# Retention branch product as seven block products per head, with tokens on partitions and the heads' sum kept on chip

## The chip, the cores and the metric

The kernel runs on one core of a Trainium2 chip. The metric is the device time of one execution in microseconds; the median of three executions before the change is 1123.46 us (1120.56 to 1124.0). A core has a matrix engine (TensorE, PE in the profile), three engines for elementwise work (VectorE or DVE, ScalarE or ACT, GpSimdE or POOL), a queue engine (SyncE, SP), and DMA engines that move data between the chip's memory and the on-chip buffers (SBUF for operands, PSUM for matmul results). Every engine works through its own instructions in the order in which they stand in its queue. In this kernel SP and POOL issue the DMAs.

## The reference

One layer of a decoder: 512 tokens, model width 1024, all fp32. A retention branch with four heads and an attention branch read the same normalised input. Cut to what the change touches:

```python
proj = h @ w_in                                  # rq, rk, rv, rg, ..., gr, gm
ro = retention(rope(rq), rope(rk) * 256**-0.5, rv)   # 4 heads, values 512 wide
ro = rms_norm(ro, ret_norm)                      # over the 512 of a head
a_ret = (ro * silu(rg)) @ w_br                   # (512 x 2048) @ (2048 x 1024)
...
mixed = sigmoid(gr) * a_ret + sigmoid(gm) * a_mla
x = x + mixed @ w_o
x = x + square(relu(rms_norm(x) @ w_up)) @ w_down
```

For one head, the branch product is a 512x512 block of `ro * silu(rg)` (tokens by values) times a 512x1024 block of `w_br`, and the four heads' products are summed.

## The kernel before

**Tiles.** Activations lie with features on the partitions and the 512 tokens along the free axis: a tile is 128x512. An fp32 product is made of three fp32r matmuls (`mm3`: high part times high part and the two mixed terms). So every operand is split into a high and a low part: ACT makes the high part by a copy (line 306 for activations, 261 for weights), DVE subtracts it for the low part (line 307 for activations, 265 or 267 for weights).

**Weights.** They come in 512 KB chunks of 128x1024. `prepare` issues a chunk's DMA on SP into one of six raw buffers (`wr_...`, line 233 or 243), `load_chunk` splits it into `wh_...` and `wl_...` (three buffers each). The list of steps in the kernel's main function sets the order of the matmuls; `run_steps` calls `load_chunk` one step ahead of use and `prepare` three further steps ahead. PE executes in the order of the list. Where the instructions of ACT, DVE, SP and POOL stand relative to one another is decided when the program is built, by a scheduler.

**Seven products.** The values (`ret_v`, tiles rv), the gates (`ret_gate`, tiles rg) and the MLP's second product cut both operands in 2x2 blocks and make the result from seven block products instead of eight, numbered 1, 7, 2, 6, 5, 4, 3 in order of use. The weights' block sums are made by DMA: the first block is loaded into a raw buffer by SP, and POOL issues a DMA that adds another block to it in place (line 223). Products 7, 6 and 4 use one raw buffer: product 6's weights are product 7's plus one more block, product 4's are product 6's plus one more. So the addition for product 6 can be issued when product 7's weights have been split, and the addition for product 4 when product 6's have. Products 1, 6, 5, 3 are accumulated in one PSUM area (chain a: the result is read out after each of them), 7 and 4 in a second one, 2 in a third one (`CHAIN`). `seven_out` reads them out: ACT copies after products 1, 7 and 6 (tiles z.._11, z.._22, z.._21 for the gates), DVE adds after 2, 5 and 4.

**Order of one head.** rq and rk (two chunks each), for even heads rv (14 chunks, values of two heads), the branch product of the previous head, gates 1 and 7, scores (`ret_scores`, tiles rs and s), gates 2 and 6, `ret_attend` (tiles ath and atl are the split scores, ro the result, og its scaled copy), gates 5, 4 and 3. During heads 0 and 2 the gate's products stand between rv or the branch product and the next head's rq.

**Branch product before.** `ret_factor` broadcasts the norm's factor of each token over the partitions with four small transposes (tile pbo), multiplies and splits the gated result into `rog`. `branch_r` makes eight output tiles of 128 features by 512 tokens, in four chunks of `w_br`, each tile of 4 x 3 matmuls of 128x512. For heads 0 to 2, ACT copies each tile (line 861) and a DMA on POOL writes it to (head 0) or adds it into (heads 1, 2) a buffer in the chip's memory, `ret{n}d`. `reload` brings the sums back as `re`, with the attention's part `ze` and the gate inputs `ge`; for head 3 DVE adds the product to `re` (line 867).

**End of the mixer.** `mix` multiplies by the gate, adds the attention's part and splits the sum into `mix{n}` (three DVE operations, lines 897, 898 and 307); `out_part` makes the first halves of two output tiles wo0 and wo1, `out_proj` the rest.

## Time and profile before

| what | value |
|---|---|
| median of three executions | 1123.46 us |
| the profiled execution | 1125.78 us |
| its span, first to last instruction | 1124.0 us |
| PE busy | 1107.5 us, 99% |
| DVE busy | 734.9 us, 65% |
| ACT busy | 536.7 us, 48% |
| weights and other reads | 156.92 MB, written 15.99 MB |

The profile gives the busy time of each engine, the chain of work that ended last (followed backwards from the last instruction), groups of equal instructions, and DMA issues with the time from issue to landing. The trace behind it gives, for each engine, a timeline: start in us, duration in us, engine, line, operation, result and operands, how often it repeats, and in brackets the idle time before it and what ended that. The line number of nearly all matmuls is that of one helper (168), so they are told apart by the tile that they write. Durations of matmuls overlap: one starts before the one ahead has ended, so the distance from start to start is what a matmul costs.

### The profile page before, as it was taken

The numbers are of one execution on the slowest core, as the hardware profiler recorded it, in microseconds if no ns is written. First come the engines' busy times: TensorE is split into PE (matmuls) and PEld (weight loads), VectorE is DVE, ScalarE is ACT, GpSimd is POOL, SyncE is SP. The second block draws the span as 40 slices with busy tenths as digits, with TensorE's granted clock in tenths as the row PEclk, the third lists the DMA queues.
The fourth block names the chain that finished last, engine by engine and source line by source line (L and its number), as shares of the span: only waits on it lengthen the run. The fifth ranks groups of instructions, "written<-read, shape, count | busy, mean of one in ns | idle before, by whom it ended". The sixth has DMA issues, their size and how long they took to land.

```text
span 1124.0 us, 14722 instructions
## 1 busy us (share of the span) xinstructions
PE 1107.5 (99%) x5549; PEld 939.0 (84%) x5549; DVE 734.9 (65%) x1206; ACT 536.7 (48%) x762; POOL 85.4 (8%) x113
## 2 busy tenths in 40 slices
PE   9999999999999999999999999999999999999998
PEld 7878878888888889888888987888888888888877
DVE  7777677556785836845483678555466666668675
ACT  7457556444465435445443644434443443445542
POOL 0000000001110020031003000010100100101000
PEclk9999999999999999999999999999999999999999
DMA  8133231356786274599529754693855755738501
GB/s 264 59 98 106 67 99 57 128 210 211 190 225 173 87 212 121 135 202 253 137 92 220 223 172 154 196 274 117 171 165 168 176 166 155 186 123 219 146 29 75
DMA packets 59223, 175.97 MB, mean 157 GB/s; under 512 B 7248, under 2 KB 8656, under 8 KB 58896
## 3 DMA queue, kind: packets, MB, share of 16 engines
q1 hardware_dynamic: 45168, 129.66, 33.8%
q0 software_dynamic: 13840, 45.36, 20.9%
q8 instruction: 43, 0.70, 0.2%
q14 instruction: 28, 0.23, 0.1%
q10 hardware_dynamic: 144, 0.03, 0.0%
HBM read 156.92 MB, written 15.99 MB: 154 GB/s over the span
## 4 chain that ended last, share of the span: by engine, by line
PE 87%; DVE 4%; DMA 4%; ACT 2%; issue 2%; SPq 0%; ACTq 0%; DVEq 0%; POOLq 0%
PE up L168 16%; PE dn L168 14%; PE br L168 6%; PE rg L168 5%; PE rv L168 5%; PE pg L168 4%; PE gr L168 4%; PE rq L168 4%; PE rk L168 4%; PE bm L168 4%; PE wo L168 4%; DMA wr_rg<-wstream 4%; PE gm L168 3%; PE ro L168 3%; PE sc L168 2%
## 5 line engine op out<-in xcount | busy, mean ns | idle before, releaser
L168 PE MATMUL dn<-wh_dn,cl 128*128 128x512 f32 x224 | 87.2, 389 | 0.0
L168 PE MATMUL dn<-wh_dn,ch 128*128 128x512 f32 x224 | 87.2, 389 | 0.0
L168 PE MATMUL dn<-wl_dn,ch 128*128 128x512 f32 x224 | 87.1, 389 | 0.0
L261 ACT ACTIVATE wh_dn<-wr_dn 128x1024 fp32r<-128x1024 f32 x32 | 34.0, 1062 | 75.5 <-PE up L168 54.3
L261 ACT ACTIVATE wh_up<-wr_up 128x1024 fp32r<-128x1024 f32 x32 | 33.9, 1061 | 57.4 <-PE up L168 29.3
L265 DVE TENSOR_TENSOR wl_dn<-wr_dn,wh_dn 128x1024 fp32r<-128x1024 f32 x32 | 39.0, 1220 | 27.5 <-ACT wh_dn L261 27.5
L265 DVE TENSOR_TENSOR wl_rg<-wr_rg,wh_rg 128x1024 fp32r<-128x1024 f32 x20 | 24.3, 1223 | 40.7 <-ACT wh_rg L261 40.4
L265 DVE TENSOR_TENSOR wl_up<-wr_up,wh_up 128x1024 fp32r<-128x1024 f32 x32 | 39.1, 1222 | 17.4 <-ACT wh_up L261 17.4
L970 DVE SCALAR_TENSOR_TENSOR f<-up,bcx 128x512 f32<-128x512 f32 x32 | 20.6, 685 | 44.1 <-PE up L168 44.1
L168 PEld LDWEIGHTS dn<-wl_dn,ch 128*128 128x128 f32 x224 | 42.0, 188 | 8.8
L168 PEld LDWEIGHTS dn<-wh_dn,cl 128*128 128x128 f32 x224 | 42.0, 188 | 8.7
L168 PEld LDWEIGHTS dn<-wh_dn,ch 128*128 128x128 f32 x224 | 42.0, 188 | 8.6
L261 ACT ACTIVATE wh_dn<-dr_dn 128x1024 fp32r<-128x1024 f32 x24 | 25.5, 1060 | 42.2 <-PE up L168 29.1
L223 POOL DMA_DIRECT2D dr_dn<-wstream x24 | 21.4, 892 | 306.3 <-DMA dr_dn<-wstream 182.0
L265 DVE TENSOR_TENSOR wl_dn<-dr_dn,wh_dn 128x1024 fp32r<-128x1024 f32 x24 | 29.3, 1222 | 22.4 <-ACT wh_dn L261 22.4
L261 ACT ACTIVATE wh_rv<-wr_rv 128x1024 fp32r<-128x1024 f32 x28 | 29.6, 1058 | 28.7 <-PE rv L168 11.8
L261 ACT ACTIVATE wh_rg<-wr_rg 128x1024 fp32r<-128x1024 f32 x28 | 29.3, 1054 | 28.9 <-DMA wr_rg<-wstream 23.6
L265 DVE TENSOR_TENSOR wl_br<-wr_br,wh_br 128x1024 fp32r<-128x1024 f32 x16 | 19.5, 1219 | 21.6 <-ACT wh_br L261 21.6
L1028 DVE TENSOR_TENSOR d<-d,dn 128x1024 f32<-128x1024 f32 x24 | 29.2, 1219 | 6.5 <-PE dn L168 6.5
L265 DVE TENSOR_TENSOR wl_rv<-wr_rv,wh_rv 128x1024 fp32r<-128x1024 f32 x20 | 24.4, 1223 | 13.6 <-ACT wh_rv L261 13.6
L861 ACT ACTIVATE rt<-br 128x512 f32<-128x512 f32 x24 | 14.3, 596 | 36.1 <-PE br L168 30.9
L644 ACT ACTIVATE p<-p,ng,hr 128x128 f32<-128x128 f32 (+3 forms) x32 | 20.6, 646 | 15.6 <-DVE ng L642 15.5
(1820 smaller groups left out, 3618.9 us busy)
## 6 DMA issues: line engine op xcount, KB each, us to landing
wr_up<-wstream SPq DMA_DIRECT2D x32, 512.0 KB, 4.4
wr_dn<-wstream SPq DMA_DIRECT2D x32, 512.0 KB, 3.4
dr_dn<-wstream POOLq DMA_DIRECT2D x24, 512.0 KB, 7.6
wr_rv<-wstream SPq DMA_DIRECT2D x20, 512.0 KB, 4.1
wr_rg<-wstream SPq DMA_DIRECT2D x20, 512.0 KB, 4.6
wr_rv<-wstream POOLq DMA_DIRECT2D x16, 512.0 KB, 6.1
wr_rg<-wstream POOLq DMA_DIRECT2D x16, 512.0 KB, 7.7
wr_br<-wstream SPq DMA_DIRECT2D x16, 512.0 KB, 3.5
```

What stands on the lines that cost most here:

```text
L168: return tc.keep_in_program_order(nc.tensor.matmul(*a, **k))
L223: nc.gpsimd.dma_start(raw, chunk(("w", blk, kb, fb, c)), accum_op=ALU.add)
L261: i = ACT(hi, raw, AF.Copy, scale=sign)
L265: TT(lo, raw, hi.bitcast(F32), op=ALU.subtract)
L644: ACT(cols[b], cols[b], AF.Exp, bias=ng[:, b:b + 1], scale=d["rq"][:, b], accum_out=sums[:, b:b + 1])
L861: ACT(t, ps, AF.Copy)
L970: STT(u[:, i], ps[:, i], 0.0, V["bcx2"], op0=ALU.max, op1=ALU.mult)
L1028: TT(to, to, dps[p], op=ALU.add if sign > 0 else ALU.subtract)
```

## The change

The operands change places: the gated retention output, tokens on the partitions of the result, becomes the stationary operand, and the weights the moving one. Each head's branch product becomes seven block products of 2 x 2 x 3 = 12 matmuls of 128x512. DVE makes the operands' block sums and splits them (`branch_operand`, two products ahead of use), and reads the result out of PSUM with one operation that multiplies by the token's factor (now a value per partition) and adds into one of eight SBUF tiles `ret[b, n]` (for head 0's first contributions ACT writes them). The weights of `w_br` come as chunks of the seven-product kind: per head five loads by SP and four adding DMAs by POOL instead of four loads. The sums stay on chip until the end, where 32 transposes on PE (`ret_turn`, tiles tr) turn them back for `mix`. To make room, the values of the odd heads are written to the chip's memory (`aside`, on POOL) and loaded again (`odd_v`, on SP, tiles cv) ahead of their use. The steps of a head's branch product are interleaved with the next head's rq and rk; head 2's rv, which had the branch product of head 1 between its chunks, now stands by itself.

```diff
-NDYN, NKEEP, NW, NRAW, NDRAW, AHEAD, PREP, EARLY, PAD = 45, 16, 3, 6, 4, 1, 3, 5, 104
+NDYN, NKEEP, NW, NRAW, NDRAW, AHEAD, PREP, EARLY, PAD = 47, 16, 3, 6, 4, 1, 3, 5, 72
...
-        for k in range(4):
-            add(("br", h, k), "w_br", _rng(h * RV, RV), _rng(2 * k * P, 2 * P))
...
+                add(("w", ("br", h), kb, fb, 0), "w_br", _rng(h * RV + kb * 256, 256), _rng(fb * S, S))
...
+                    if blk % 10 == 1:
+                        v[j] = split(t, f"rv{q}{blk}{i}")
+                        continue
+                    if blk == 12:
+                        t = T(f"cv{q}{i}_12")
+                        ACT(t, rvps[ch][i], AF.Copy)
+                    v[j] = aside(f"v{q}{j}", t)
+
+    def odd_v(h):
+        for j in range(4):
+            t = T(f"cv{h}{j}")
+            nc.sync.dma_start(t, R[h]["v"][j])
+            R[h]["v"][j] = split(t, f"rv{h}{j}")
...
+        R[h]["nr"] = sm(f"nro{h}", keep=True)
+        TS(R[h]["nr"], R[h]["r"], -1.0, None, op0=ALU.mult)
...
-    def ret_factor(h):
-        d, r = R[h], R[h]["r"]
-        bc = bcast(B(f"pbo{h}"), lambda b: r[:, b:b + 1])
-        for m in range(4):
-            TT(d["og"][m], d["og"][m], bc, op=ALU.mult)
-            new = K if m < 2 and h < RH - 1 else T
-            d["rog"][m] = split(d["og"][m], None, hi=new(f"rog{h}{m}h", F32R), lo=new(f"rog{h}{m}l", F32R))
-
-    def branch_r(w, h, half):
+    def branch_operand(h, p):
+
+        (a, b), lo_, hi_ = R[h]["o"], slice(0, 256), slice(256, 512)
+        if p == 7:
+            R[h]["s"] = T(f"bs{h}")
+        sv = two(R[h]["s"]) if "s" in R[h] else None
+        if p in (1, 2, 4):
+            src = (a if p == 1 else b)[:, :, hi_ if p == 4 else lo_]
+        elif p == 5:
+            src = two(T(f"bt{h}"))
+            TT(src, a[:, :, hi_], b[:, :, hi_], op=ALU.subtract)
+        else:
+            src = sv
+            if p == 7:
+                TT(sv, a[:, :, hi_], a[:, :, lo_], op=ALU.subtract)
+            else:
+                TT(sv, b[:, :, hi_ if p == 6 else lo_], sv, op=ALU.subtract)
+        hi, lo = two(T(f"bx{h}{p}h", F32R)), two(T(f"bx{h}{p}l", F32R))
+        split(src, None, hi=hi, lo=lo)
+        R[h]["x", p] = [(hi[:, k], lo[:, k]) for k in range(2)]
...
+    def branch_r(w, h, p):
+
+        ch, d = CHAIN[p], R[h]
+        if p in (1, 7, 2):
+            brps[ch] = [B(f"br{h}{p}{i}") for i in range(2)]
+        for k in range(2):
+            for i in range(2):
+                mm3(brps[ch][i], cut(d["x", p][k], i * P), cut(w, k * S, S), p in (1, 7, 2) and k == 0, k == 1,
+                    skip_group_check=True)
...
         for i in range(2):
-            n = 2 * half + i
-            ps = proj(B(f"br{h}{n}"), R[h]["rog"], w, i * P, 2 * P)
-            if h < RH - 1:
-                t = T(f"rt{h}{n}")
-                ACT(t, ps, AF.Copy)
-                if h == 0:
-                    ret[n] = aside(f"ret{n}", t)
-                else:
-                    nc.gpsimd.dma_start(ret[n], t, accum_op=ALU.add)
+            b, n = 2 * (to // 10 - 1) + i, to % 10 - 1
+            r, ps = d[f][:, b:b + 1], brps[ch][i]
+            if h == 0 and p in (1, 7, 6, 3):
+                ret[b, n] = T(f"ret{b}{n}")
+                ACT(ret[b, n], ps, AF.Copy, scale=r)
             else:
-                TT(ret[n], ret[n], ps, op=ALU.add)
+                STT(ret[b, n], ps, r, ret[b, n], op0=ALU.mult, op1=ALU.add)
+
+    def ret_turn(n):
+
+        trp[n] = B(f"tr{n}")
+        for b in range(4):
+            MM(trp[n][:, b * P:b * P + P], ret[b, n // 4][:, n % 4 * P:n % 4 * P + P], ident, is_transpose=True,
+               start=b == 0, stop=b == 3, skip_group_check=True)
...
-        TT(ret[n], ret[n], sgr[n], op=ALU.mult)
-        TT(ret[n], ret[n], zm[n], op=ALU.add)
-        mixed[n] = split(ret[n], f"mix{n}")
+        TT(sgr[n], trp[n], sgr[n], op=ALU.mult)
+        TT(sgr[n], sgr[n], zm[n], op=ALU.add)
+        mixed[n] = split(sgr[n], f"mix{n}")
...
+    def branch_steps(h, seq):
+
+        order = [p for p in seq if not callable(p)]
+        for p in seq:
+            if callable(p):
+                p()
+                continue
+            step(("sw", ("br", h), p, 0), branch_r, h, p)
+
+            for p2 in order[order.index(p) + 2:order.index(p) + 3]:
+                step(None, branch_operand, h, p2)
+
     for h in range(RH):
...
+        if h:
+            branch_steps(h - 1, [1, qk("rq", 1), 7, 2, qk("rk", 0), 6, 5, qk("rk", 1), 3, 4])
...
+        if h % 2:
+            step(None, odd_v, h)
...
         step(None, ret_gated, h)
+        for p in (1, 7):
+            step(None, branch_operand, h, p)
     for n in range(8):
         step(None, reload, n)
-    for n in range(EARLY, 8):
-        step(("gr", n), gate_r, n)
-        if n == EARLY:
-            step(None, ret_factor, RH - 1)
-    for k in range(4):
-        step(("br", RH - 1, k), branch_r, RH - 1, k)
-        step(None, mix, 2 * k)
-        step(None, mix, 2 * k + 1)
+    step(("gr", 5), gate_r, 5)
+    branch_steps(RH - 1, [1, 7, lambda: step(("gr", 6), gate_r, 6), 2, 6, 5, 4, 3])
+    for n in range(4):
+        step(None, ret_turn, n)
+        step(None, mix, n)
+    step(("gr", 7), gate_r, 7)
+    for n in range(4, 8):
+        step(None, ret_turn, n)
+        step(None, mix, n)
     for n in range(2):
         step(("o", n), out_part, n, 0)
```

Three places show what this does to the engines' queues. In them a name ends in the number of its buffer, and a name of the gates carries the head and the product: `wh_rg160` is the high part of head 1's weights for product 6.

The first is ACT's queue in head 1, from gate product 2's weights to the scores' splits. Before:

```order
L261 ACTIVATE wh_rg120_4257<-wr_rg120_4189 128x1024
L742 ACTIVATE z1_11_4255<-rg11_4230 128x512
L261 ACTIVATE wh_rg160_4337<-wr_rg170_4148 128x1024
L742 ACTIVATE z1_22_4289<-rg17_4264 128x512
L261 ACTIVATE wh_rg150_4371<-wr_rg150_4261 128x1024
L306 ACTIVATE ath_85<-s10_4300 128x512
L306 ACTIVATE ath_85<-s11_4311 128x384
L306 ACTIVATE ath_85<-s12_4322 128x256
L306 ACTIVATE ath_85<-s13_4333 128x256
L261 ACTIVATE wh_rg140_4474<-wr_rg170_4148 128x1024
```

The same place now, where `rv10h` to `rv13h` are the high parts of the values that were loaded again:

```order
L305 ACTIVATE rv10h_4222<-cv10_4220 128x512
L260 ACTIVATE wh_rg160_4356<-wr_rg170_4181 128x1024
L260 ACTIVATE wh_rg150_4390<-wr_rg150_4280 128x1024
L305 ACTIVATE rv11h_4228<-cv11_4226 128x512
L305 ACTIVATE rv12h_4234<-cv12_4232 128x512
L260 ACTIVATE wh_rg140_4491<-wr_rg170_4181 128x1024
L305 ACTIVATE rv13h_4240<-cv13_4238 128x512
L741 ACTIVATE z1_11_4274<-rg11_4249 128x512
L741 ACTIVATE z1_22_4308<-rg17_4283 128x512
L305 ACTIVATE ath_85<-s10_4319 128x512
```

The copy of gate product 1 (`z1_11`) stood ahead of the weights of product 6; now it, and all splits of the scores behind it, stand behind the weights of product 4 (`wh_rg140`), which are in the raw buffer only after both adding DMAs. Head 3's queue reads the same, with `z3_11` directly behind `wh_rg340`.

The four `cv` loads stand on SP among the weight loads, each behind one that waits for a raw buffer.

The second is ACT's queue in head 0, around the splits of its scores. Before:

```order
L306 ACTIVATE ath_85<-s00_3575 128x512
L306 ACTIVATE ath_85<-s01_3586 128x384
L306 ACTIVATE ath_85<-s02_3597 128x256
L261 ACTIVATE wh_rg040_3749<-wr_rg070_3459 128x1024
L306 ACTIVATE ath_85<-s03_3608 128x256
```

Now:

```order
L305 ACTIVATE ath_85<-s00_3571 128x512
L305 ACTIVATE ath_85<-s01_3582 128x384
L305 ACTIVATE ath_85<-s02_3593 128x256
L305 ACTIVATE ath_85<-s03_3604 128x256
L260 ACTIVATE wh_rg040_3743<-wr_rg070_3455 128x1024
```

The fourth split no longer stands behind product 4's weights. In head 2 it did before and still does.

The third is DVE's queue at the start of the output product, where `wl_o_1` is the low part of the second chunk of `w_o`. Before:

```order
L898 TENSOR_TENSOR re6_6376<-re6_6376,ze6_6378 128x512
L897 TENSOR_TENSOR re7_6380<-re7_6380,gr7_6506 128x512
L265 TENSOR_TENSOR wl_o_1_6700<-wr_o_1_6697,wh_o_1_6699 128x1024
L307 TENSOR_TENSOR mix6l_6688<-re6_6376,mix6h_6687 128x512
L898 TENSOR_TENSOR re7_6380<-re7_6380,ze7_6382 128x512
```

Now:

```order
L943 TENSOR_TENSOR ge4_6408<-tr4_6728,ge4_6408 128x512
L943 TENSOR_TENSOR gr5_6445<-tr5_6740,gr5_6445 128x512
L306 TENSOR_TENSOR mix3l_6692<-ge3_6404,mix3h_6691 128x512
L944 TENSOR_TENSOR ge4_6408<-ge4_6408,ze4_6406 128x512
L944 TENSOR_TENSOR gr5_6445<-gr5_6445,ze5_6410 128x512
L943 TENSOR_TENSOR gr6_6533<-tr6_6751,gr6_6533 128x512
L306 TENSOR_TENSOR mix4l_6737<-ge4_6408,mix4h_6736 128x512
L944 TENSOR_TENSOR gr6_6533<-gr6_6533,ze6_6412 128x512
L306 TENSOR_TENSOR mix5l_6748<-gr5_6445,mix5h_6747 128x512
L943 TENSOR_TENSOR gr7_6726<-tr7_6762,gr7_6726 128x512
L306 TENSOR_TENSOR mix6l_6759<-gr6_6533,mix6h_6758 128x512
L944 TENSOR_TENSOR gr7_6726<-gr7_6726,ze7_6414 128x512
L264 TENSOR_TENSOR wl_o_1_6776<-wr_o_1_6773,wh_o_1_6775 128x1024
```

Twelve operations of 512 columns, of which the first reads the transposes tr4 behind gate product 7, now stand ahead of `wl_o_1`, whose use on PE comes 12 matmuls after the last transpose (tr7).

More of the change, by code (lines that the diff above doesn't have):

```diff
@@ L566, in rotary_out @@
         for i in range(4):
[L567 removed]
+            t = dyn.tile([P, S], F32R, tag="t", name=f"qp{gq}{i}")
             for j, srct in enumerate((h1, h2, l1, l2)):
@@ L691, in branch_m @@
         zm[n] = aside(f"am{n}", t)
-    ret, sgr, mixed = [None] * 8, [None] * 8, [None] * 8
-    R = [dict(rog=[None] * 4, og=[]) for _ in range(RH)]
+    ret, sgr, mixed = {}, [None] * 8, [None] * 8
+    R = [dict() for _ in range(RH)]
     xr, xn, XS = [], [], {}
@@ L799, in ret_attend @@
         d = R[h]
+        d["o"] = [dyn.tile([P, 2, S], F32, tag="o2", name=f"og{h}{k}", bufs=2) for k in range(2)]
         for m in range(4):
@@ L869, in reload @@
+    trp = {}
+    def ret_turn(n):
[3 more added lines that the diff above has]
+               start=b == 0, stop=b == 3, skip_group_check=True)
     def reload(n):
-        for l, nm in ((ret, "re"), (zm, "ze"), (sgr, "ge")):
+        for l, nm, new in ((zm, "ze", K), (sgr, "ge", T)):
             if l is sgr and n >= EARLY:
                 continue
-            t = K(f"{nm}{n}")
+            t = new(f"{nm}{n}")
```

34 lines of the change are left out of this document (16 added, 18 removed).

## The prediction

> **What bounds the kernel now.** I read the page first, then the waits of PE, then PE's timeline in the stage that the change touches.
>
> ```profile
> span 1124.0 us, 14722 instructions
> PE 1107.5 (99%) x5549; PEld 939.0 (84%) x5549; DVE 734.9 (65%) x1206; ACT 536.7 (48%) x762; POOL 85.4 (8%) x113
> PE 87%; DVE 4%; DMA 4%; ACT 2%; issue 2%; SPq 0%; ACTq 0%; DVEq 0%; POOLq 0%
> PE ro L168 <- ACT ath L306: 2.3, 2, 1.7
> PE ro L168 <- DVE atl L307: 1.8, 2, 0.9
> PE wo L168 <- DVE wl_o L265: 0.5, 1, 0.5
> ```
>
> PE is busy 99% of the span and is 87% of the chain. So time is won by taking matmuls away, and lost wherever PE, which now waits for almost nothing, begins to wait. The waits (total, times, longest) list no wait for the branch product; in the mixer they are the two for `ro` and one for `wo`. The profiled execution took 1125.78 us, 1.78 more than its span and 2.32 more than the median of 1123.46; I sum against the first and carry the difference over to the second.
>
> **Work that PE loses and gains.**
>
> ```profile
> 396.97 21.76 PE br L168 x96
> 652.66 0.60 PE L168 MATMUL pbo<-cst,ro 128*128 128x128 f32 x4
> 653.02 0.48 PE L168 MATMUL gr<-xn0h,wl_gr 128*128 128x512 f32 x1
> 1060.83 1.75 PE tr L168 x16
> ```
>
> One head's branch product is 96 matmuls in 21.76 us, 0.227 us each (chain of waits). It becomes 7 x 12 = 84; the moving operand stays 512 wide. Four heads lose 48 matmuls: 48 x 0.227 = **-10.9 us**. The transposes of `ret_factor` go: from 652.66 to 653.02 is 0.36 us a head, **-1.4**. The 32 transposes of `ret_turn` are like the tail's `tr`, 16 in 1.75 us: **+3.5**. Work on PE: **-8.8 us**.
>
> **Head 0: a wait that goes.** The listed waits for `ro` are in heads 0 and 2, where the fourth score split stands on ACT behind product 4's weights, which wait for an adding DMA.
>
> ```profile
> 356.19 1.06 ACT L261 ACTIVATE wh_rg<-wr_rg 128x1024 fp32r<-128x1024 f32 x1 [2.19 <-DMA wr_rg<-wstream]
> 357.15 0.40 ACT L306 ACTIVATE ath<-s 128x256 fp32r<-128x256 f32 x1
> 357.60 0.38 PE L168 MATMUL ro<-ath,rv0211l 128*128 128x256 f32 x1 [0.70 <-ACT ath L306]
> 358.89 0.38 PE L168 MATMUL ro<-atl,rv0211h 128*128 128x256 f32 x1 [0.91 <-DVE atl L307]
> 434.13 7.71 PE ro L168 x48
> ```
>
> Head 1's `ro` without a wait takes 7.71 us. In head 0, from 356.63 to 357.60 and from there to 358.89 two matmuls of 0.12 take 2.26, so 2.0 to 2.1 us are lost. The queue now has all four splits ahead of those weights: **-2.1 us**. Head 2 keeps its place in the queue: **0**.
>
> **Head 1: a wait that comes.** In the order now, ACT has the copy `z1_11` behind `wh_rg140`. PE cannot begin gate product 6 before that copy, since both use one PSUM area (chain a).
>
> ```profile
> 421.69 0.60 ACT L742 ACTIVATE z<-rg 128x512 f32<-128x512 f32 x1 [1.33 <-issue]
> 431.33 1.06 ACT L261 ACTIVATE wh_rg<-wr_rg 128x1024 fp32r<-128x1024 f32 x1 [1.36 <-PE rg L168]
> 418.57 0.28 PE L168 MATMUL rg<-xn0h,wl_rg 128*128 128x256 f32 x1
> 431.08 0.28 PE L168 MATMUL rg<-s60h,wl_rg 128*128 128x256 f32 x1
> ```
>
> Before, the copy ran at 421.69, right after product 1, and the weights of product 4 were split at 431.33, released by PE: with three `wh` buffers they wait for the end of product 2. Product 6 began 431.08 - 418.57 = 12.5 us after product 1, straight after product 2. Now even with no delay by DMA, ACT after that end has `wh_rg140` (1.0), `rv13h` (0.6) and `z1_11` (0.6) to do: a **floor of 2.2 us** in which PE stands. The DMAs can add to it. Product 6's addition waits until product 7's weights are split; counting DVE's queue from rk's last matmul, that is at 0.1 us after product 1's start. Then come its landing L1, the two halves of the split (1.06 and 1.22, here 2.2), product 4's addition and its landing L2. So `wh_rg140` can start at 0.1 + L1 + 2.2 + L2, and waits beyond the floor if L1 + L2 is over 10.2.
>
> ```profile
> wr_rg<-wstream POOLq DMA_DIRECT2D x1, 512.0 KB, 6.8
> wr_rg<-wstream POOLq DMA_DIRECT2D x1, 512.0 KB, 5.5
> ...
> wr_rg<-wstream POOLq DMA_DIRECT2D x1, 512.0 KB, 5.2
> wr_rg<-wstream POOLq DMA_DIRECT2D x1, 512.0 KB, 5.3
> ...
> wr_rg<-wstream POOLq DMA_DIRECT2D x1, 512.0 KB, 8.6
> wr_rg<-wstream POOLq DMA_DIRECT2D x1, 512.0 KB, 5.8
> ...
> wr_rg<-wstream POOLq DMA_DIRECT2D x1, 512.0 KB, 8.1
> wr_rg<-wstream POOLq DMA_DIRECT2D x1, 512.0 KB, 5.5
> ```
>
> These are the pairs (product 6, product 4) of heads 0 to 3, issue to landing. Their sums are 12.3, 10.5, 14.4 and 13.6, mean 12.7. By the mean the stall is 2.2 + 2.5 = 4.7; ends 2.2 and 6.4. I take the mean, not head 1's own 10.5, because four reloads of 256 KB now share this stage: **+4.7 us**. The reloaded values `rv12`, `rv13` stand in the same queue, each behind a weight load on SP; by the sum they land about when L2 ends, and are no term of their own.
>
> **Head 3** has `z3_11` directly behind `wh_rg340`: floor 1.6, and by the same mean about **+4.7 us**. Before, heads 1 and 3 lost nothing there.
>
> **The output product: a wait that grows.** `wl_o_1` now stands behind twelve operations of `mix`, the first of which needs the transposes tr4 that follow the last gate product.
>
> ```profile
> 675.78 0.68 DVE L898 TENSOR_TENSOR re<-re,ze 128x512 f32<-128x512 f32 x1
> 676.39 0.68 DVE L897 TENSOR_TENSOR re<-re,ge 128x512 f32<-128x512 f32 x1
> 676.99 1.22 DVE L265 TENSOR_TENSOR wl_o<-wr_o,wh_o 128x1024 fp32r<-128x1024 f32 x1
> 678.12 0.68 DVE L307 TENSOR_TENSOR mix2l<-re,mix2h 128x512 fp32r<-128x512 f32 x1
> ```
>
> One such operation costs 0.60 from start to start, a weight's low part 1.13. After the gate product's end, tr4 takes 0.44 (a quarter of 1.75), the twelve 7.2, `wl_o_1` 1.2: 8.8 us. PE has tr4 to tr7 (1.75) and 12 matmuls of `wo0` (2.72): 4.5 us. Stall 4.4; before, PE lost 0.5 to 0.8 there: **+3.7 us** (ends 3 and 5).
>
> **VectorE in the branch product.** Per head DVE gets seven weight splits instead of four, seven operand splits, four subtractions and fourteen read-outs, and loses eight operations of `ret_factor`.
>
> ```profile
> 374.00:451.00 77.00, 77.00 (x449) 68.63 (x449) 46.76 (x80) 35.02 (x50) 7.91 (x12) 1.00 0.50 148
> ```
>
> Head 1's stretch had DVE busy 46.76 of 77 us (third pair), so the average has room. But between rq's second chunk and the last product, PE has 84 + 72 matmuls = 35.4 us, and DVE's queue has 13 operations of 1024 and 33 of 512 columns, 13 x 1.13 + 33 x 0.60 = 34.5. Nearly full, and in fixed order: I take 0.6 us a head for three heads, **+1.8** (ends 0 and 12, where every operation starts late by the order).
>
> **TensorE's clock after a stall.** In head 2, PE waited for `ro` too:
>
> ```profile
> 552.07 0.39 PE L168 MATMUL ro<-ath,rv1211l 128*128 128x256 f32 x1 [1.65 <-ACT ath L306]
> 553.86 0.63 PE L168 MATMUL ro<-ath,rv1110l 128*128 128x512 f32 x1
> 554.29 0.63 PE L168 MATMUL ro<-atl,rv1110h 128*128 128x512 f32 x1
> 557.18 0.40 PE L168 MATMUL ro<-ath,rv1110l 128*128 128x512 f32 x1
> 557.41 0.40 PE L168 MATMUL ro<-atl,rv1110h 128*128 128x512 f32 x1
> ```
>
> After it a matmul cost 554.29 - 553.86 = 0.43 us until about 557, and 0.23 from 557.18: 12 matmuls took 3.3 us instead of 1.9. So a stall of 3 us cost 1.4 more; head 0's of 2 us cost nothing. I take 1.0 for each of the three new stalls: **+3.0** (ends 0 and 5). The Trainium skill, "TensorE: Matmul & The Clock Gate", Part 1, says that an idle window of about 3.4 us halves the clock and that about 3.4 us of work restore it, in a window that runs freely. The pace here agrees (0.43 against 0.23), though the listed idle pieces before it are 1.65 and 0.91 us, shorter than that window. By that rule each stall over 3.4 us costs an estimated 1.7, and the term would be 5.1 instead of 3.0.
>
> **Sum.** -8.8 - 2.1 + 4.7 + 4.7 + 3.7 + 1.8 + 3.0 = **+7.0 us**: 1132.8 for an execution like the profiled one, 1123.46 + 7.0 = 1130.5 as the median. I say 1130.5.
>
> **Rivals.**
>
> *The waits shrink to their floors* (not slower). Place: ACT's queue in heads 1 and 3; it decides if L1 + L2 is at most 10.2 there. Then -8.8 - 2.1 + 2.2 + 1.6 + 3.7 + 0.9 + 1.0 = -1.5: 1122. For it: head 1's own pair of 10.5, and DMAs that are rarer once `ret` stays on chip. Against: three of four pairs are at 12.3 or above.
>
> *All of it is covered* (faster). If ACT and DVE reach these places early enough that PE never stands, only PE's work and head 0's wait count: 1123.46 - 10.9 = 1112.6. Against: the floor follows from the order and from the end of product 2, not from a DMA.
>
> *DMAs slow down* (slower). Odd heads' values go out and come back, 8 tiles of 256 KB each way, and the branch weights need adding DMAs. With 8.6 for each landing L1 + L2 is 17.2: stalls of 9 us in heads 1 and 3, and head 2's wait grows by some 3: 1130.5 + 8.6 + 3 = 1142.
>
> *VectorE paces the branch product* (slower). If its operations start in order and late, 3 to 4 us a head, its term is 12 instead of 1.8: 1141. For it: 34.5 of 35.4 us; against: weight splits run ahead of use.
>
> **How the numbers follow.** Chances: forecast 0.45 (its own range 1125 to 1138), floors 0.20, all covered 0.13, DMAs 0.11, VectorE 0.11. A measurement of this kernel can tell about 0.3% or 3.4 us from no change: 1120.1 to 1126.8 is "same". Faster: 0.13 and a fifth of the floors' case, 0.17. Same: the rest of the floors' case and a tenth of the forecast's, 0.21. Slower: 0.62. The range leaves out the covered case and the far half of the two slow ones: 1116 to 1141.
>
> **What would show it.** Right: PE idle before head 1's first `rg<-s60h`, released by ACT's z, 2 us or more, and the same in head 3; no wait for `ro` in head 0; PE idle before `wo` for `wl_o` of some 4 us; the last adding DMA of a head landing 10 us or more after the first was issued. Wrong: `z1_11` done before product 2 ends; matmuls of `br` further apart than 0.23 us over a whole head (VectorE); or `tr` slower than 0.11 us each.

## Result and the profile after

The changed kernel takes 1163.85 us (median, 1162.8 to 1166.05), the kernel before 1123.73 in the same series: ratio 1.036 with a 95% interval of 1.0336 to 1.0391. It is slower by 40 us, where the prediction said 7, and outside its range of 1116 to 1141. The page, and then the waits of PE (total, times, longest), read:

```profile
span 1161.8 us, 14724 instructions
PE 1110.2 (96%) x5517; PEld 937.3 (81%) x5517; DVE 783.7 (67%) x1258; ACT 548.5 (47%) x774; POOL 85.9 (7%) x113
PE 49%; DMA 7%; DVE 4%; issue 2%; ACT 1%; POOL 0%; SPq 0%; ACTq 0%; POOLq 0%; DVEq 0%
PE rg L167 <- ACT z L741: 17.4, 3, 9.9
PE rk L167 <- DVE wl_rk L264: 5.8, 2, 3.1
PE wo L167 <- DVE wl_o L264: 4.6, 1, 4.6
PE pbk L167 <- DVE hr L604: 3.1, 2, 2.3
PE br L167 <- DVE ret L904: 2.3, 3, 1.3
```

PE has 32 instructions fewer and yet 2.7 us more of busy time, since matmuls after a long wait run slower (the rows below show it; the granted clock of the run is 0.985 against 0.997). In the chain that ended last PE's share fell from 87 to 49%, and DMA's rose from 4 to 7%. The waits for z and for the weights of rk were not in the list before; the one in wo was 0.5 us, the one for pbk 0.8. The spans differ by 37.8 us; PE's timeline, cut into stages by what it writes, gives where (the second branch row holds head 2's rv):

| stage | before | after | difference |
|---|---|---|---|
| up to the first rq (attention) | 279.34 | 283.37 | +4.03 |
| head 0 to its gates | 95.21 | 92.82 | -2.39 |
| branch of head 0, rq and rk of head 1 | 44.02 | 41.24 | -2.78 |
| head 1, gates, scores, ro | 32.63 | 41.20 | +8.57 |
| branch of head 1, rq, rk, rv of head 2 | 82.09 | 87.68 | +5.59 |
| head 2, gates, scores, ro | 37.27 | 36.38 | -0.89 |
| branch of head 2, rq and rk of head 3 | 44.01 | 47.27 | +3.26 |
| head 3, gates, scores, ro | 32.63 | 44.94 | +12.31 |
| gr, branch of head 3, tr | 38.57 | 40.40 | +1.83 |
| wo | 44.36 | 51.98 | +7.62 |
| the rest | 393.87 | 394.52 | +0.65 |

**Heads 1 and 3, gates.** PE's rows where gate product 6 begins, in head 1 and in head 3:

```profile
436.50 0.58 PE L167 MATMUL rg<-s60h,wl_rg 128*128 128x256 f32 x1 [6.39 <-ACT z L741]
...
652.79 0.58 PE L167 MATMUL rg<-s60h,wl_rg 128*128 128x256 f32 x1 [9.88 <-ACT z L741]
653.17 0.41 PE L167 MATMUL rg<-s60l,wh_rg 128*128 128x256 f32 x1
653.38 0.41 PE L167 MATMUL rg<-s60h,wh_rg 128*128 128x256 f32 x1
...
655.93 0.28 PE L167 MATMUL rg<-s60h,wh_rg 128*128 128x256 f32 x1
656.05 0.28 PE L167 MATMUL rg<-s60h,wl_rg 128*128 128x256 f32 x1
```

It is the place and the releaser that the prediction named. The stage loses more than the idle time: after 9.88 us matmuls of 256 columns start 0.21 us apart at first, and 0.12 from 655.93; the granted clock is 0.50 from 652.8 to 655.9 and 1.00 behind it. What z stood behind is in ACT's rows, of head 1 first and then of head 3:

```profile
433.87 0.63 ACT L305 ACTIVATE rv12h<-cv 128x512 fp32r<-128x512 f32 x1 [7.30 <-DMA cv<-v02d]
434.40 1.04 ACT L260 ACTIVATE wh_rg<-wr_rg 128x1024 fp32r<-128x1024 f32 x1
435.35 0.61 ACT L305 ACTIVATE rv13h<-cv 128x512 fp32r<-128x512 f32 x1
435.87 1.07 ACT L741 ACTIVATE z<-rg 128x512 f32<-128x512 f32 x2
...
651.20 1.06 ACT L260 ACTIVATE wh_rg<-wr_rg 128x1024 fp32r<-128x1024 f32 x1 [7.70 <-DMA wr_rg<-wstream]
652.16 1.07 ACT L741 ACTIVATE z<-rg 128x512 f32<-128x512 f32 x2
```

In head 1 the last to come is the reloaded value cv12, in head 3 the weights of product 4. The issues behind them, on SP and POOL (issue time first):

```profile
427.51 0.33 SPq L232 DMA_DIRECT2D wr_br<-wstream  x1
427.93 0.40 SPq L779 DMA_DIRECT2D cv<-v02d  x1
...
417.85 0.85 POOL L222 DMA_DIRECT2D wr_rg<-wstream  x1 [7.26 <-DVE wl_rg L264]
426.65 0.86 POOL L222 DMA_DIRECT2D wr_rg<-wstream  x1 [7.95 <-DVE wl_rg L264]
...
633.49 0.86 POOL L222 DMA_DIRECT2D wr_rg<-wstream  x1 [10.72 <-DVE wl_rg L264]
643.89 0.89 POOL L222 DMA_DIRECT2D wr_rg<-wstream  x1 [1.94 <-issue]
```

Head 1's additions landed after 6.1 and 5.6 us, the second by 432.3; cv12, issued behind a weight load of the branch that had waited for a buffer, came 5.9 us after 427.93, 1.6 later still. In head 3 the additions took 6.8 and 7.2.

**Branch product.** Head 1's, on POOL, ACT, DVE and PE, at the wait for rk (and the same in head 2):

```profile
470.03 0.86 POOL L222 DMA_DIRECT2D wr_br<-wstream  x1 [10.63 <-issue]
...
477.44 1.06 ACT L260 ACTIVATE wh_br<-wr_br 128x1024 fp32r<-128x1024 f32 x1 [2.43 <-DMA wr_br<-wstream]
478.40 0.61 ACT L305 ACTIVATE rqy2h<-rqb 128x512 fp32r<-128x512 f32 x1
...
479.05 0.69 DVE L306 TENSOR_TENSOR rqy2l<-rqb,rqy2h 128x512 fp32r<-128x512 f32 x1 [2.18 <-ACT rqy2h L305]
479.66 1.22 DVE L264 TENSOR_TENSOR wl_rk<-wr_rk,wh_rk 128x1024 fp32r<-128x1024 f32 x1
...
480.93 0.50 PE L167 MATMUL rk<-xn0h,wl_rk 128*128 128x512 f32 x1 [3.07 <-DVE wl_rk L264]
```

To be read upwards: rk waits for the low part of its weights; on DVE that stands behind rqy2l, which needs rqy2h; on ACT that stands behind the branch weights of product 6, which wait for an adding DMA issued at 470.03. DVE itself was idle for 2.18 us. So rk, which has nothing to do with those weights, waits for their DMA through two queues. The Trainium skill, "TensorE: Matmul & The Clock Gate", section "Architectural detail: the array is 16× 32×32, not 1× 128×128", calls ACT's and DVE's queues strict FIFO; these rows agree (rqy2h ran only behind the 2.43 us wait of the row ahead).

**Start of wo, and attention.** The transposes and the wait in wo; then the place where attention lost its 4 us, on ACT and on PE:

```profile
713.63 1.91 PE L167 MATMUL tr<-cst,ret 128*128 128x128 f32 x16
715.30 0.48 PE L167 MATMUL wo<-mix0h,wl_o 128*128 128x512 f32 x1
...
722.88 0.76 PE L167 MATMUL wo<-mix0h,wl_o 128*128 128x512 f32 x1 [4.60 <-DVE wl_o L264]
...
159.44 0.47 ACT L308 ACTIVATE v21h<-pv,f 128x256 fp32r<-128x256 f32 x1 [3.17 <-DMA qp<-qr11h]
...
163.52 1.12 PE L167 MATMUL pbk<-cst,hr 128*128 128x128 f32 x8 [2.25 <-DVE hr L604]
```

Sixteen transposes take 1.67 us from start to start. The value copy v21h got the buffer of qr11h, which the last DMA into a qp tile was still reading: the change moved qp into the pool `t`.

### The profile page after: what moved, and what is told of

It is laid out like the page before. It is cut to its first block, busy times and chain, and to the rows that moved or that the text cites. A ratio compares the mean times of both kernels' runs of the same rounds, so it can differ in the third digit from the quotient of the medians.

```text
span 1161.8 us, 14724 instructions
## 1 busy us (share of the span) xinstructions
PE 1110.2 (96%) x5517; PEld 937.3 (81%) x5517; DVE 783.7 (67%) x1258; ACT 548.5 (47%) x774; POOL 85.9 (7%) x113
## 4 chain that ended last, share of the span: by engine, by line
PE 49%; DMA 7%; DVE 4%; issue 2%; ACT 1%; POOL 0%; SPq 0%; ACTq 0%; POOLq 0%; DVEq 0%
PE up L167 15%; PE dn L167 13%; PE pg L167 4%; PE wo L167 3%; PE rg L167 3%; PE br L167 2%; PE rk L167 2%; DMA wr_rg<-wstream 2%; DMA wr_br<-wstream 2%; PE ro L167 2%; PE gr L167 1%; DMA wr_rv<-wstream 1%; PE rq L167 1%; PE pw L167 1%; DMA v13d<-cv 1%
## 5 line engine op out<-in xcount | busy, mean ns | idle before, releaser
L260 ACT ACTIVATE wh_br<-wr_br 128x1024 fp32r<-128x1024 f32 x28 | 29.6, 1059 | 25.8 <-DMA wr_br<-wstream 8.9
L264 DVE TENSOR_TENSOR wl_rv<-wr_rv,wh_rv 128x1024 fp32r<-128x1024 f32 x20 | 24.4, 1224 | 17.4 <-ACT wh_rv L260 15.9
L222 POOL DMA_DIRECT2D wr_br<-wstream x16 | 14.2, 887 | 174.6 <-DVE wl_br L264 53.3
```

The costliest lines, as they stand in the source:

```text
L222: nc.gpsimd.dma_start(raw, chunk(("w", blk, kb, fb, c)), accum_op=ALU.add)
L260: i = ACT(hi, raw, AF.Copy, scale=sign)
L264: TT(lo, raw, hi.bitcast(F32), op=ALU.subtract)
```

## Experiments

Times below are to be compared with 1163.85 and with the kernel before of the same series (1121.3 to 1124.2). Runs without an interval are single executions. In the diffs `behind(i, j)` only fixes that `i` stands behind `j` in its queue; it adds no semaphore.

**1. Product 4's weights behind the scores.**

```diff
         i = ACT(hi, raw, AF.Copy, scale=sign)
+        if key[0] == "sw" and key[1][0] == "rg" and key[2] == 4:
+            behind(i, <ACT's last ath split of this head>)
```

> Only ACT's order is changed: in each head the high part of gate product 4's weights is queued behind the four splits of the scores; the reloaded values stay where they are. Changed kernel: gate products 2 and 6 take 14.33 us in head 1 and 17.25 in head 3 (5.76 without a wait). Theory A (the wait is for product 4's adding DMA): head 3 falls to about 7 us, since rv33h was done at 643.4 and product 6 could begin at about 644; head 1 only by 1 to 2 us, since there rv12h (landed 433.87) stood just as late. Total about 1163.85 - 10 - 1.5 = 1152 us. Theory B (the reloads of the values are the wait): both stay within 2 us, total 1160 to 1164.

1153.28 us. Head 3's row:

```profile
643.57 0.39 PE L167 MATMUL rg<-s60h,wl_rg 128*128 128x256 f32 x1 [1.28 <-ACT z L746]
```

The wait of 9.88 is 1.28, the second gate group 7.29 instead of 17.25 us. Head 1 keeps 5.63 of its 6.39. So head 3 waited for the addition, and head 1, once that is out of the way, still waits for the reload.

**2. The reloads a step later as well** (the step `odd_v` behind gate products 1 and 7).

> As the run before, and the odd heads' values are reloaded and split after gate products 1 and 7 in the program, so that ACT's copy z of gate product 1 gets its buffer and its place ahead of them. Theory A (ACT's queue and the buffers decide, the DMAs are early enough for their own users): gate products 2 and 6 take 5.8 to 6.5 us in heads 1 and 3, ro waits 0 to 3 us for the last value; total about 1163.85 - 8.5 - 11.5 + 2 = 1146 us. Theory B (DMA is short in this stage): the wait moves to ro with nearly its size, total above 1158 us.

1158.93 us. The wait has moved from z to `ro`; head 3's row (head 1's is 4.17):

```profile
652.44 0.80 PE L167 MATMUL ro<-ath,rv30l 128*128 128x512 f32 x1 [11.01 <-ACT ath L310]
```

The score splits now stand behind late values. That is the time of theory B, but not its reason: run 7 moves the same data without such a wait. Issuing a reload later only makes it late.

**3. Product 6's branch weights in written order.**

```diff
-        if key[0] == "a1":
+        if key[0] == "a1" or key[0] == "sw" and key[1][0] == "br" and key[2] == 6:
             tc.keep_in_program_order(i)
```

> Only ACT's order: the high part of branch product 6's weights is queued behind the splits of rq. Changed kernel: rk's first chunk comes 3.2 us late in head 1's branch phase and 2.9 in head 2's, then runs at the slow pace; the phases lose 8.7 and 6.3 us over their 44 matmul groups' own time, rv included. Theory A (rqy's split behind a weight that waits for its adding DMA holds DVE's queue and so the weights of rk): these two waits go, total about 1163.85 - 10 = 1154 us. Theory B (VectorE's queue is too long, whatever the order): PE waits as long for another of DVE's results, total above 1160 us.

1163.7 us: no gain in all, though the wait for rk is 0.80 instead of 3.07 and the stretch from branch product 7 to product 5, with half of rk in it, takes 18.0 us instead of 22.1 (head 1) and 21.7 (head 2). The mechanism is shown; the same queues, filled otherwise, lost as much elsewhere: attention +1.6, the gates and `ro` of heads 1 to 3 +3.7, the last branch stage and wo +3.1.

**4. Half of the mix behind the first output chunk.**

```diff
-    for n in range(2):
-        step(("o", n), out_part, n, 0)
+    step(("o", 0), out_part, 0, 0)
+    for n in range(4, 8):
+        step(None, mix, n)
+    step(("o", 1), out_part, 1, 0)
```

(and `mix` 4 to 7 leave the loop of `ret_turn`.)

> Only the order at the end of the mixer: the first half of output tile 0, and with it the split of the second chunk of w_o, come ahead of mix 4 to 7 in the program. Changed kernel: wo takes 51.98 us (43.5 without a wait), 4.6 of it waiting for wl_o. Theory A (wl_o_1 behind twelve mix operations, and the clock falls in that wait): wo takes 44 to 45.5 us, total about 1163.85 - 7 = 1157 us. Theory B (the mix operations are the path): PE waits for the last mix instead, wo takes 49 us or more, total above 1160 us.

1160.45 us; wo takes 46.46 instead of 51.98 us, its wait 1.03 instead of 4.60. Attention came 1.9 later in this build, which eats a third of it.

**5. qp in the pool of kept tiles.** `t = K(f"qp{gq}{i}", F32R)` in place of the tag `t`.

> Only the buffers of the attention's query tiles qp: they come from the pool of kept tiles (which has free places there) instead of the pool t of 47. Changed kernel: retention begins (first rq matmul) at 283.37 us, before the change at 279.34; PE waits 2.25 us for pbk, because the split v21h writes the buffer of qr11h, which the last qp DMA still reads. Theory A (the pool t is short of buffers, and the attention pays for it): retention begins at 279 to 281 us, total about 1163.85 - 3.5 = 1160 us, everything later as before. Theory B (the order of the sixteen qp DMAs is the cause): still 283 us or later.

1156.8 us. The retention begins at 276.83 instead of 283.37 (279.34 before). The wait of v21h stands in the traces of runs 1, 3, 4 and 9, which leave qp in `t`, and in none of those that move it (runs 5, 8 and 10). The attention loss was the buffer.

**6 and 7. Reloads ahead of the loads that they stood behind; and that with edit 1.**

```diff
-            nc.sync.dma_start(raw, chunk(("w", blk, kb, fb, c)))
+            i = nc.sync.dma_start(raw, chunk(("w", blk, kb, fb, c)))
+            behind(i, <cv1 ahead of branch product 1's chunk, cv3 ahead of 7's and of rq1's>)
```

> Only SP's order: in heads 1 and 3 the loads of the values are queued ahead of the weight loads for the next rq chunk and the branch products. Changed kernel: gate products 2 and 6 take 14.33 and 17.25 us. Theory A (two waits stand in the same queue, the values' loads and product 4's adding DMA, and either alone is enough): head 1 stays at 13 to 14.5 us, since z1_11 is still behind wh_rg14; in head 3 z3_11 is now ahead of wh_rg34 but the splits of the scores are behind it, so products 2 and 6 take 6 to 8 us and ro 15 or more. Total 1160 to 1166. Theory B (the loads alone make the wait): both heads come down to 6 to 8 us and ro stays at 8, total about 1145.

> Both: the values' loads ahead of the weight loads, and product 4's weights behind the splits of the scores. Theory A: both waits are gone, gate products 2 and 6 take 5.8 to 7.5 us and ro 7.7 to 8.5 in heads 1 and 3, total about 1163.85 - 8 - 10.5 = 1145 us. Theory B (DMA is short in this stage): products 2 and 6 or ro still wait 4 us or more in head 1, total above 1151.

1161.14 and 1145.98 us. Alone it helps little, since product 4's weights still stand ahead of z in head 1, where the second gate group is 13.89; head 3's falls to 10.29, but `ro` then waits 3.06 us for the splits of the scores. With both, it is 5.82 and head 3's 7.06, and PE's wait for z reads:

```profile
PE rg L167 <- ACT z L755: 2.7, 2, 1.7
```

17.4 us of waiting for z are 2.7. In head 1 either cause alone was enough to hold z, so both had to go; in head 3 the addition was the one that counted (run 1).

**8. All five edits** (1, 3, 4, 5 and 6).

> All the edits that touch order and buffers only: the two of the run before, the branch weights of product 6 behind rq's splits, the chunk of w_o ahead of mix 4 to 7, qp in the other pool. The arithmetic is that of the changed kernel. Theory A (the waits are separate, each goes with its edit): 1163.85 - 8 - 10.5 (gates) - 7.5 (branch phases) - 5.5 (wo) - 3.5 (attention) = 1129 us. Theory B (the pool of 47 buffers is the common cause, and a wait taken away comes back elsewhere, as the gain of the branch phases did): 1138 us or more.

1130.27 us, near theory A's 1129; ratio to the kernel before 1.0075 (1.0056 to 1.0094). 33.6 of the 40 us are gone by the order of queues and one pool, with the arithmetic unchanged. Head 2's gates (9.61 for 5.76) and the last branch stage (16.85 for 13.6) are the largest losses left.

**9. The values of odd heads kept on chip.** The change's aside and reload undone, with the loads of `ze` held in written order on SP:

```diff
-                    if blk % 10 == 1:
-                        v[j] = split(t, f"rv{q}{blk}{i}")
-                        continue
-                    ...
-                    v[j] = aside(f"v{q}{j}", t)
+                    new, nm = T if blk % 10 == 1 or i else K, f"rv{q}{blk}{i}"
+                    v[j] = split(t, None, hi=new(nm + "h", F32R), lo=new(nm + "l", F32R))
...
-        if h % 2:
-            step(None, odd_v, h)
```

> The changed kernel without its aside and reload of the odd heads' values: the four value tiles of an odd head are split at once and their halves stay on chip until the head's last product, half of them in the pool of kept tiles; the sums of sqrt(d) tiles and orders are otherwise those of the change. Theory A (the gates of heads 1 and 3 wait because the reloads and their elementwise copies stand in the queues between the products, and because the accumulation of product 4 comes before z): without reloads z stands ahead of that accumulation in heads 1 and 3, the second gate group of both takes 5.8 to 7.3 us as in the run with both orders instead of 14.3 and 17.3, and the time falls by 16 to 19 us, to 1145 to 1148. Theory B (the reason is the number of tiles alive at once): kept values leave fewer buffers for operands, the waits turn up elsewhere (branch products, products of rk, attention), and the time stays above 1155.

1140.02 us, 23.8 less: more than expected. The second gate groups take 5.76 and 5.88, head 2's stage too is free of its wait for z, and no `rg <- ACT z` stands among PE's waits:

```profile
PE rk L167 <- DVE wl_rk L264: 5.9, 2, 3.0
PE wo L167 <- DVE wl_o L264: 4.6, 1, 4.6
PE pbk L167 <- DVE hr L604: 3.1, 2, 2.3
PE br L167 <- DVE ret L899: 2.6, 3, 1.6
```

Branch, wo and attention waits stay, so keeping the values did not push them elsewhere (theory B). One edit of the change, made for room that could be found in the other pool, is 24 of its 40 us: the reloads, and an order of the queues that was built around them. (The edit also holds the `ze` loads in order; what that alone does was not tried.)

**10. Kept values and the four other orders.**

> The kernel with the kept values of the run before, plus four of the orders: product 4 of the gates behind the scores, product 6 of the branch in written order, the first output chunk ahead of the second half of the mix, and the qp tiles in the other pool. Theory A (the losses add and each has its own cause): what the run with all five orders gave, 1130, or up to 4 us less because head 3 has no reload in its way: 1126 to 1131. Theory B (buffers): the two uses of the kept pool (values, qp tiles) collide, attention or a branch stage grows by 5 us or more: above 1134.

1122.83 us, ratio 0.998 (0.9956 to 1.0004): below what was expected, and equal to the kernel before.

**11 and 12. Two of the head sums in the kept pool, and then the mix's additions on GpSimd** (both on the kernel of run 8).

> All five orders, and the two head sums of the first output column (two of the eight ret tiles) in the kept pool, so that the pool of 47 has two buffers more. Theory A (what is left in head 2, 4.8 us in its gates, is a shortage of two buffers): head 2's second gate group falls from 9.6 to about 7.5 us, the time from 1130.3 to 1127 or 1128. Theory B (the accumulating transfers alone set it): head 2 stays at 9 to 10 us and the time at 1129 to 1132.

> As the run before, and the eight additions of the attention part in the mix run on GpSimd in place of VectorE. Theory A (in the last branch stage, 16.9 us for 13.6 of work, and in front of wo VectorE paces): the last branch stage and wo together lose 2 to 4 us against the run before, 1124 to 1126. Theory B (the stage waits for operands whose transfers are late, not for VectorE): no difference above 1 us; or GpSimd is slower on its additions than VectorE was and wo starts later: 1 to 3 us slower.

1124.11 and 1125.75 us, ratios 1.0007 (0.9988 to 1.0027) and 1.0011 (0.9991 to 1.0032). With two buffers freed, head 2's second gate group went from 9.61 to 5.76. Whether the buffers themselves did it or the order that the scheduler chose with them was not separated. On GpSimd an addition takes longer; in run 12 and, on VectorE, in run 11 (five of the eight: busy, mean ns):

```profile
L959 POOL TENSOR_TENSOR ge<-ge,ze 128x512 f32<-128x512 f32 x5 | 7.2, 1469 | 18.4 <-DVE ge L958 14.3 <-DMA wr_o<-wstream 4.1
```

```profile
L959 DVE TENSOR_TENSOR ge<-ge,ze 128x512 f32<-128x512 f32 x5 | 3.4, 689 | 0.0
```

wo grows from 46.3 to 50.0 us; the last branch stage hardly moves (17.1 to 16.8). Theory A's gain does not come; since the addition itself takes twice as long there, this does not show whether VectorE's queue paces wo.

**13. Product 6 ahead of product 2** (on run 10, in every head). In heads 0 to 2 the additions for product 6 are then issued ahead of the split of product 7's weights, so there product 7 computes with weights to which product 6's block has already been added; the work is the same. Run 16 has this too.

> The kernel with kept values and four orders, and in every head product 6 of the branch ahead of product 2 (1, 7, 6, 2, 5, 4, 3), so that the products 6 and 5, which add up in one pair of banks, have another product between them. Theory A (in the branch stages TensorE waits 0.26 us in heads 1 and 2 and 1.0 us in the last one for VectorE to have read the banks between 6 and 5, and then goes at the slow pace): these waits on ret go, the last branch stage falls from 16.95 to 15 us or less, the stage behind rk from 6.0 to 5.5, in all 2 to 3.5 us. Theory B (VectorE as a whole is late there): the wait moves to the next operand or weight, less than 1 us is won.

1131.98 us. The part that was meant holds: no wait on ret, the last branch stage 14.73 instead of 16.95, the stage behind rk 5.44 instead of 5.94. But in heads 0 to 2 new waits of 2.3 to 3.0 us in all come at the start of product 6; in head 1, on ACT and PE:

```profile
465.20 0.63 ACT L310 ACTIVATE rqx2h<-rqa 128x512 fp32r<-128x512 f32 x1 [5.40 <-DVE rqa L792]
...
466.34 1.04 ACT L260 ACTIVATE wh_br<-wr_br 128x1024 fp32r<-128x1024 f32 x1
...
467.44 0.51 PE L167 MATMUL br<-wh_br,bx16l 128*128 128x512 f32 x1 [1.53 <-ACT wh_br L260]
```

Product 6, now needed earlier, has its weights still behind rq's splits, where edit 3 had put them.

**14 and 15. Head 3's statistics behind gate product 4; a third output column's first half ahead** (each on run 10).

> The same base, and in head 3 the statistics of the heads' output stand behind product 4 of the gates instead of ahead of it. Theory A (the 0.91 us of waiting for sqo in head 3 and the slow pace behind it, 2.6 us in all, come from ScalarE's late squares and nothing needs the statistics earlier): the gates of head 3 after ro take 9.5 instead of 12.2 us and the time falls by 2 to 3 us. Theory B (the factor is needed right after): ret of product 1 and so the branch stage waits, no gain.

> The same base, and the first half of output column 2 also runs ahead of the second half of column 0's sum, so that wo has 2.7 us more work before it needs mix4 to mix7. Theory A (wo waits 1.55 us for the last tiles of the mix, and pays 1.3 us of slow pace): wo falls from 46.4 to 44 us, the time by 2 to 3 us. Theory B (its weights' third chunk, prepared by VectorE in the same stretch, is the next wait): wo stays at 46 us or grows.

1118.91 and 1127.05 us. In run 14 the gates behind head 3's `ro` take 9.5 instead of 12.2 us, as expected. In run 15 wo grows to 50.9, as theory B had it: now it is the third chunk's low part that stands behind the mix, as the second's did in the changed kernel, on DVE and PE:

```profile
687.45 1.22 DVE L267 TENSOR_TENSOR wl_o<-wr_o,wh_o 128x1024 fp32r<-128x1024 f32 x1
...
688.81 0.77 PE L167 MATMUL wo<-mix0h,wl_o 128*128 128x512 f32 x1 [4.16 <-DVE wl_o L267]
```

**16. The three together.**

> The three edits together on the base of 1122.8. Theory A (the places are independent): 6 to 9 us less, 1114 to 1117, faster than the kernel before by 0.5 to 0.8%. Theory B (they share VectorE and what is won in one stage is lost in the next): 1119 to 1123, no difference from the kernel before.

1135.86 us, ratio 1.0121 (1.0093 to 1.0149): the new waits of 13 and 15 come together, and the gain of 14 stays.

**17. The two places that held.**

> The base of kept values and four orders, with the statistics of head 3 behind product 4 and, in the last head alone, product 6 ahead of product 2 (there a gate of the attention part stands between 7 and 6, so that product 7's weights are split before the next chunk is added to them). Theory A (the places are independent, each worth what its stage showed): the last branch stage takes 14.2 to 14.8 us, the gates behind ro in head 3 9.5 us, wo 46.4 us as before it, in all 4.5 to 6 us less than the base: 1116 to 1119, 0.3 to 0.5% faster than the kernel before. Theory B (VectorE as a whole): wo begins earlier and waits longer for the mix, wo grows by 2 us or more, 1120 to 1123, no difference from the kernel before.

1118.41 us, ratio 0.995 (0.9936 to 0.9964): half a per cent below the kernel before, a small gain with 1 outside its interval. The last branch stage takes 14.46, head 3's gates behind `ro` 9.5, wo 48.0 (46.4 expected). The page:

```profile
span 1119.7 us, 14692 instructions
PE 1100.8 (98%) x5517; PEld 928.9 (83%) x5517; DVE 783.1 (70%) x1258; ACT 544.9 (49%) x770; POOL 81.2 (7%) x105
```

## Why the prediction was wrong

Its direction, three of its terms and the places of three waits were right; its size was not. Every sign that it named for being right is in the trace, and none of those for being wrong: none of them looked at the rk matmuls between the branch products, where much of the time went. By its own steps, in the profiled executions:

| term | predicted | in the traces |
|---|---|---|
| PE's work | -8.8 | -9.0 (worked out from the pace of the rows: three branch stages 3.08 less, the last 0.25 more) |
| head 0, wait for `ro` | -2.1 | -2.1 (`ro` 9.84 to 7.71) |
| head 1, gates | +4.7 | +6.4 idle |
| head 3, gates | +4.7 | +9.9 idle |
| start of wo | +3.7 | +4.1 idle (4.60 less 0.55) |
| branch stages beyond PE's work ("VectorE") | +1.8 | +16.9 |
| slow clock after the three stalls | +3.0 | +8.2, all that these stages lost beyond the idle time; 4.9 of it by the slow pace |
| attention | none | +4.0 |

The rows add up to 38.4; with -0.3 from the other matmuls of head 0, -0.9 from head 2 and +0.6 from the rest they give the 37.8 of the spans.

**The step that failed most** is the one on the branch product. "VectorE in the branch product" counted DVE's operations against PE's time, found 34.5 of 35.4 us and took 0.6 us a head. Load was not the matter: from rq's second chunk to rv, DVE was busy 30.64 of 38.37 us in head 1, and ahead of the wait for rk it was idle. What counted most is the queue ahead of it: an ACT instruction that waits for an adding DMA holds everything behind it, on ACT and through it on DVE. I had used that very rule for the gates, and did not carry it to the branch product, which has the same kind of weights, four adding DMAs a head. At the start of rk this cost 9.7 of the 16.9 us against the matmuls' own pace (5.0 in head 1, 4.7 in head 2, slow matmuls included), and run 3 takes 7.8 of them back. It also shows that a better order at one place alone is paid back at others; in runs 8 and 10, where it comes with the rest, it is kept. Of the other 7 us, 2.8 are waits of product 5 for the read-outs of product 6, which share a PSUM area (in run 13, with another product between them, they are gone), 3.0 lie in head 2's rv and 1.0 ahead of head 3's gates, in short waits for DVE and ACT that were not tried one by one. The rival "VectorE paces the branch product" was nearer, with a term of 12 for operations that start in order and late, but its ground, a full queue, is not what the trace shows.

**The stalls of heads 1 and 3** had the right mechanism and the wrong size. In head 1 the rule of two landings gives 6.1 + 5.6 = 11.7, near the 12.7 taken. What was wrong is "by the sum they land about when L2 ends, and are no term of their own": the reload cv12 came 1.6 us after the addition, and runs 1, 6 and 7 show that either alone holds z (second gate group 13.49 with the reload alone, 13.89 with the addition alone, 5.82 with neither). For head 3 the prediction's own working, floor 1.6 and 2.5 beyond it, gives 4.1, not the 4.7 that it took. In head 3 product 6's addition was issued 3.5 us after product 1's start (633.49 against 629.96), not the 0.1 of the prediction: it waits for the low part of product 7's weights, and on DVE that stood behind two read-outs of the branch product and the low part of a reloaded value:

```profile
629.83 1.40 DVE L904 SCALAR_TENSOR_TENSOR ret<-br,nro,ret 128x512 f32<-128x512 f32 x2
631.14 0.68 DVE L306 TENSOR_TENSOR rv30l<-cv,rv30h 128x512 fp32r<-128x512 f32 x1
631.74 2.36 DVE L264 TENSOR_TENSOR wl_rg<-wr_rg,wh_rg 128x1024 fp32r<-128x1024 f32 x2
```

The landings, 6.8 and 7.2, and 3.6 instead of 2.2 us for the splits between them, do the rest. Run 9 settles the common cause: without the reloads both stalls go, although product 4 is added by DMA as before, because z is then queued ahead of it.

**The slow clock** was taken at 1.0 a stall. What the stages lost beyond the idle time is 2.2 in head 1 (8.57 - 6.39), 2.4 in head 3 (12.31 - 9.88) and 3.6 in wo (7.62 - 4.05). Not all of that is the clock: by the rows at the slow pace (436.87 to 440.72, 653.17 to 655.93, 723.44 to 727.66; granted clock 0.50) it took 1.7, 1.2 and 2.0 us. Of wo's rest, 1.1 us is a new wait for xr at its end. The Trainium skill, "TensorE: Matmul & The Clock Gate", Part 1, puts half speed behind an idle window of about 3.4 us, and about 3.4 us of work until it ends, an estimated 1.7 a stall: nearer to 1.7, 1.2 and 2.0 than my 1.0. Yet the pace fell to 0.43 us also behind rk's waits of 3.07 and 2.76 us, shorter than that window.

**Attention** was left out, because the diff moves only one name there. That line moved qp from six buffers of its own into the common pool `t`, and another tile's first write then waited for a DMA (run 5).

**Where the gain went.** PE's saved work and the score waits of heads 0 and 2 are 15.7 us; run 10 has them, and won 1.8 by its span. The stages say why. Against their matmuls' own pace they lose 1.6 and 2.7 in the branch stages of heads 1 and 2, 1.9 in rv, 2.9 in head 3, 3.5 in the last branch stage and 2.9 in wo, in waits of 0.2 to 1 us. Only in head 3 is the pace slow behind one (granted clock 0.50 until 635.83). At the others it stays at 0.23 us, but each costs some 0.3 us more than its listed length: around the wait of 0.80 for rk, two matmuls take 1.53 us (464.30 to 465.83) instead of 0.45, which is 1.08 lost. Runs 14 and 17 show two of them to be separate waits; for the others that was not tried. Each edit also makes the scheduler fill queues anew at places that it does not touch (head 2's second gate group took 7.18 us in the changed kernel, 9.61 in run 8, 5.76 in run 10); which of its rules does that stays open.

## What to carry to other kernels

Look, for every instruction that waits for a DMA on an elementwise engine, at what stands behind it in that queue, and follow that to the other engines; an engine's spare time says nothing about it. A tile that is written out and loaded again costs more than its transfers when its copies stand in the same queues as work on the path; look for room in another pool first. When PE is busy nearly all the time, matmuls saved count only if no new wait comes with them: in run 10, listed waits of 8.4 us in the six stages cost 15.5.

## What the runs showed of the hardware

A load of 512 KB that adds in place lands later than a plain one: medians of 6.8 against 4.7 us for the gates' weights in the changed kernel.

```profile
wr_rg<-wstream SPq DMA_DIRECT2D x20, 512.0 KB, 4.7
...
wr_rg<-wstream POOLq DMA_DIRECT2D x16, 512.0 KB, 6.8
```

TensorE's slow pace (granted clock 0.50) came after a wait of 2.76 us as after one of 9.88, and lasted 2.8 to 4.2 us. In run 10 it also came after a wait of 0.91 us with eight one-column matmuls behind it, and not after one of 1.00 us with wide ones. Where the clock stayed at 1.00, short waits cost some 0.3 us more than their listed length. An addition of 128x512 took 0.69 us on VectorE and 1.47 on GpSimd (means of five).
